# Four PSUM banks in rotation for the scan's stage of a hybrid SSD and attention layer, with eight smaller edits

## The chip, the cores and the metric

The kernel runs on one core of a Trainium2 chip: TensorE (PE) with its weight loads (PEld), VectorE (DVE), ScalarE (ACT), GpSimd (POOL), SyncE (SP, which here only issues DMAs), and 16 DMA engines. PE's sums go to PSUM, eight banks of 128 partitions by 2 KB. The metric is the device time of one execution in microseconds (us); lower is better.

## The reference

One layer of a decoder for 512 tokens of a prompt and 64 of samples (8 sequences of 8 tokens behind 2048 cached positions), 1024 wide, all in float32. Cut to what is computed:

```python
h = x + 0.5 * swiglu(rmsnorm(x, ffn1_norm), ffn1_w_gate, ffn1_w_up, ffn1_w_down)     # D_FF = 2816
xn = rmsnorm(h, mix_norm)
z, xbc, dt_raw, q, k, v, f_raw, g_ssd, g_att = split_combined(xn @ w_in)
y_ssd, h_new, conv_new = ssd_branch(z, xbc, dt_raw, conv_prev, h0, p)
...                      # rms norm of q and k; logf = log_sigmoid(f_raw + b_f)
y_att = fox_attention(q, k_all, v_all, logf_all)      # softmax(q k / 8 + sum of logf), paged past
merged = (sigmoid(g_ssd) * (y_ssd @ w_ssd_proj) + sigmoid(g_att) * (y_att @ w_attn_proj))
h = h + merged @ w_out
h = h + 0.5 * swiglu(rmsnorm(h, ffn2_norm), ffn2_w_gate, ffn2_w_up, ffn2_w_down)
```

`ssd_branch` is a causal convolution over 4 tokens with SiLU, a scan in chunks of 128 tokens (32 heads of 64 in 4 groups, state of 128), a gate SiLU(z), and an rms norm over each group's 512 channels:

```python
y_diag = einsum('bclsgr,bcsgrp->bclgrp', cb[..., None] * decay, xdt)      # cb = C.B within a chunk
states = einsum('bclgn,bclgr,bclgrp->bcgrpn', Bc, exp(acs[:, :, -1:] - acs), xdt)
h_fin, h_prev = lax.scan(step, h_init, (chunk_decay, states))
y_off = einsum('bclgn,bcgrpn,bclgr->bclgrp', Cc, h_prev, exp(acs))
```

The layer also returns keys, values, logf, the scan's final states and the convolution's last inputs.

## The kernel before

Activations lie with channels on the partitions and the 576 tokens (NT; 512 of them NP, the prompt's, and 64 NS, the samples') in the columns, in two halves of 288 (HT). A float32 product is made of three matmuls of a rounded format: weights and activations are split in a high and a low part (`whi`, `wlo`; `xh`, `xl`), and `mm3` issues hi x hi, hi x lo, lo x hi per slice of 128 inputs (L212 to L214). A half tile of a projection from 1024 inputs is 24 such matmuls.

The stages in order of time: the first FFN (from 0 to about 485 us); projections for dt, f, q, k and the rest of the attention's (to 600); attention, with the z gates' projection and others as filling jobs (`beside`, `fill`) between its steps (to 897); the mixing stage (897 to 1376), which is the scan's stage here; then `w_out` and the second FFN.

The mixing stage: `group_in(g)` makes a group's six tiles of B, C and x (`conv_tile`: two half tiles of projection on PE, scaled into `xr` by DVE at L1149 and L1154/L1156, turned at L1162, convolved with `kf` on DVE, L1175). `group_scan(g)` goes over chunk 4 (the samples' tokens) and chunks 0 to 3 with `chunk`, `carry` and `state`. For a chunk, a DMA brings `ab` (cumulated log decays, spread over the partitions, L1314), ACT makes the decay `dk` of it (L1319, L1320), DVE multiplies it by the masked product C.B (`cbm`, L1321), ACT and POOL make the carried part of `ab` (L1323, L1324); PE turns x (L1330) and B (L1337), then multiplies (L1346, L1348); `carry` adds up the state `hst` (L1359 to L1365); `state` multiplies the samples' old states, read back turned from `hTD` (L1373), into `oo`, and `gate` multiplies by z and sums squares on POOL (L1270 to L1274). `oo` is turned at the end into a tile of tag "tr" (L1393), the final state into another (L1404). `halves` splits the result into `ygh` and `ygl`. `group_out(g)` projects it: 16 half tiles of 12 matmuls, each multiplied by the group's norm from `rowscale` (L261 sums squares over partitions on PE) on DVE (`u`, L1425; or L1422) and added to `accs`. Between them stand gate tiles (three behind the first scan, five behind the last) and, first, the attention's projection of `yhl`.

The eight PSUM banks: `accp` has two (tag "acc"); "tr" (turned tiles), "mm" (`sm()`) and "pv" have two each. A tile of a tag takes the slot of the tile two before it, in the order of the program's text. `acc()` gives the accumulator of a projection; while `wide[0]` is true (first FFN, `w_out`, second FFN) every second comes from "pv". In the mixing stage all come from "acc".

The order on each engine is not written out: a scheduler places the instructions by its own times, bound by data, slots and priority (`soon()` raises it); `behind(later, first)` only fixes an order between two instructions and adds no wait. `turns` (L369) turns the samples' old SSM states during the first FFN: a load on SP's queue, four transposes on PE (L385), a copy and a store on ACT's queue. `aside` runs it behind the preparation of the past's log forget values.

Of the kernel before, what the change touches and what calls it, by code (L numbers as in the profile page):

```python
# [23 lines left out]
P = 128  # L24
# [69 lines left out]
def build(ctx, tc, A, O):  # L94
# [113 lines left out]
    def mm3(out, w, xs, half, first=True, last=True):  # L208
        n = len(w)
        for i, ((hi, lo), (xh, xl)) in enumerate(zip(w, xs)):  # L210
            a, b = xh[:, hs(half)], xl[:, hs(half)]
            mm(out, lhsT=hi, rhs=a, start=first and i == 0, stop=False)  # L212
            mm(out, lhsT=hi, rhs=b, start=False, stop=False)  # L213
            mm(out, lhsT=lo, rhs=a, start=False, stop=last and i == n - 1)  # L214

    def hilo(hp, view, tagh, tagl, scale=None, n=NT, bufs=None):

        hi = tl(hp, [P, n], F32R, tag=tagh, bufs=bufs)
        lo = tl(hp, [P, n], F32R, tag=tagl, bufs=bufs)
        if scale is None:  # L220
            act(hi, view, AF.Copy)
            V.tensor_tensor(lo, view, hi.bitcast(F32), ALU.subtract)
        else:
            act(hi, view, AF.Copy, scale=scale)  # L224
            V.scalar_tensor_tensor(lo, view, scale, hi.bitcast(F32), ALU.mult, ALU.subtract)
        return hi, lo
# [45 lines left out]
    class Norm:  # L272


        def __init__(self, wcol, sqp=None, xsp=xp):
            self.wcol, self.xs, self.n, self.sqp, self.xsp = wcol, [], 0, sqp, xsp

        def add(self, h, squares=True):
            k = self.n
            self.xs.append(hilo(self.xsp, h, "xh", "xl", scale=P1[:, self.wcol + k:self.wcol + k + 1]))  # L280
# [88 lines left out]
    def turns(wait):  # L369

        for _ in range(wait):
            yield
        with pool("turn", side="right", reuse_waits="tile") as sp_:
            tiles = []
            for t in range(16):
                for h in range(2):
                    for n in range(len(tiles), min(2 * t + h + 3, 32)):
                        tiles.append(tl(sp_, [P, 4, P], tag="h0", bufs=4))
                        nc.sync.dma_start(out=tiles[n], in_=ap3(A["state_ssm"][0], *place(n % 2, n // 2)))
                    if t + h == 0:  # L380
                        yield
                    h0 = tiles[2 * t + h]
                    ps = tr()
                    for b in range(4):
                        nc.tensor.transpose(ps[:, b * P:(b + 1) * P], h0[:, b, :], ident)  # L385
                    hT = tl(sp_, [P, 512], tag="hT", bufs=3)
                    act(hT, ps, AF.Copy)
                    nc.scalar.dma_start(out=hTD[h, t], in_=hT)
                    yield

# [27 lines left out]
    with pool("h1", reuse_waits="tile") as hp:  # L418
# [41 lines left out]
        with pool("setup2", side="right", reuse_waits="tile") as su:  # L460
# [36 lines left out]
            q.dma_start(out=bb[:32], in_=A["dt_bias"].rearrange("o h -> h o"))  # L497
            q.dma_start(out=bb[32:48], in_=A["b_f"].rearrange("o h -> h o"))
# [3 lines left out]
            q.dma_start(out=al[:32], in_=A["a_log"].rearrange("o h -> h o"))  # L502
# [14 lines left out]
        def aside():  # L517

            with pool("rows", side="right", reuse_waits="tile") as su:

                sc = tl(su, [24, CONV], tag="sc")
                for j in range(3):
                    nc.scalar.dma_start(out=sc[j * B:(j + 1) * B], in_=A["state_conv"][0, :, j, :])
                yield
                yield
                scT = tl(su, [P, 24, 24], tag="scT")
                for j in range(0, 24, 12):
                    t = tr()
                    for i in range(12):
                        nc.tensor.transpose(t[:, i * 24:(i + 1) * 24], sc[:, (j + i) * P:(j + i + 1) * P], ident[:24, :24])  # L530
                    V.tensor_copy(scT[:, j:j + 12, :], t[:, :288].rearrange("p (i c) -> p i c", c=24))
                nc.scalar.dma_start(out=scD, in_=scT)

            with pool("lg", side="right", reuse_waits="tile") as lp:
                pcol = tl(lp, [P, 1], I32, tag="pcol")
                nc.scalar.dma_start(out=pcol, in_=A["page_table"].rearrange("b n -> (b n)").unsqueeze(1))
                lg = tl(lp, [P, P, 16], tag="lg")
                G.indirect_dma_start(out=lg.rearrange("p s h -> p (s h)"), out_offset=None,
                                     in_=A["cache_logf"].rearrange("o n s h -> (o n) (s h)"),
                                     in_offset=bass.IndirectOffsetOnAxis(ap=pcol[:, :1], axis=0))  # L540
                pf = tl(lp, [P, 16, P], tag="pf")
                for h in range(16):
                    V.tensor_tensor_scan(pf[:, h, :], C("one"), lg[:, :, h], 0.0, ALU.mult, ALU.add)
                tot = tl(lp, [P, 16], tag="tot")
                V.tensor_copy(tot, pf[:, :, P - 1])
                page = tl(lp, [P, P], tag="page")
                nc.scalar.dma_start(out=page, in_=A["consts"][:, COFF["page"][0]:COFF["page"][0] + P])
                for _ in range(2):
                    yield
                t = sm()  # L550
                mm(t[:, :16], lhsT=page, rhs=tot, start=True, stop=True)
                st = tl(lp, [P, 16], tag="st")
                V.tensor_copy(st, t[:, :16])

                for h in range(16):
                    G.tensor_tensor(lg.rearrange("p s h -> p (s h)")[:, h * P:(h + 1) * P].rearrange("p (q r u) -> p r q u", q=4, u=4),
                                    pf[:, h, :].rearrange("p (r q u) -> p r q u", q=4, u=4),
                                    st[:, h:h + 1].unsqueeze(2).unsqueeze(3).to_broadcast([P, 8, 4, 4]), ALU.subtract)
                lv = lg.rearrange("p s h -> p (s h)").rearrange("p (h q e) -> p h q e", h=16, q=4)
                for b in range(B):  # L560
                    for q in range(4):
                        nc.scalar.dma_start(out=pastD[b, :, q].rearrange("h g e -> g h e"), in_=lv[b * NPG:(b + 1) * NPG, :, q, :])
            yield from turns(1)
# [12 lines left out]
    wide[0] = False  # L576
# [79 lines left out]
    with pool("att", side="right", reuse_waits="tile") as ap:  # L656
# [147 lines left out]
        G.memset(qz, 0.0)  # L804
        t = sm()
        for j in range(8):
# [3 lines left out]
            mm(t[:, j * NS:(j + 1) * NS], lhsT=sel, rhs=hr[:, NP:], start=True, stop=True)  # L810
# [211 lines left out]
        def beside():  # L1022
            jobs = [(ga, j) for j in range(8)] + [(zc, j) for j in range(16)]
            ahead = ga.get(0)
            for n, (cols, j) in enumerate(jobs):
                w, ahead = ahead, None
                v = tl(mixp, [P, NT], tag="kf", bufs=2)
                for half in range(2):
                    a = acc()
                    for k in range(0, 8, 4):  # L1030
                        mm3(a, w[k:k + 4], xs[k:k + 4], half, first=k == 0, last=k == 4)
# [16 lines left out]
                yield  # L1048

        filler = beside()  # L1050
# [479 lines left out]
```

## Time and profile before

| what | us |
|---|---|
| runs: median of three (lowest, highest) | 1869.34 (1866.79, 1869.46) |
| the profiled execution, its span | 1870.09, 1868.2 |
| PE, its weight loads busy | 1824.8, 1725.6 |
| DVE, ACT, POOL busy | 1064.6, 742.1, 605.7 |
| stage 600 to 897 (attention), PE busy | 297.0, 295.73 |
| stage 1376 to the end, PE busy | 492.2, 486.56 |

The profile lists each engine's instructions with start and length; the groups' names are `out<-in` by the program's tiles, with the line that issued them. The waits view adds up, for one engine, the idle time ahead of a line's instructions and what ended it: us in total, times, longest. The granted clock is 0.995 of full speed in the mean. Matmuls are pipelined and their ends are modelled, so a row can be longer than the distance to the next start.

### The profile page before, as it was taken

The numbers are of one execution on the slowest core, as the hardware profiler recorded it, in microseconds if no ns is written. First come the engines' busy times: TensorE is split into PE (matmuls) and PEld (weight loads), VectorE is DVE, ScalarE is ACT, GpSimd is POOL, SyncE is SP. The second block draws the span as 40 slices with busy tenths as digits, with TensorE's granted clock in tenths as the row PEclk, the third lists the DMA queues.
The fourth block names the chain that finished last, engine by engine and source line by source line (L and its number), as shares of the span: only waits on it lengthen the run. The fifth ranks groups of instructions, "written<-read, shape, count | busy, mean of one in ns | idle before, by whom it ended". The sixth has DMA issues, their size and how long they took to land.

```text
span 1868.2 us, 38772 instructions
## 1 busy us (share of the span) xinstructions
PE 1824.8 (98%) x15335; PEld 1725.6 (92%) x15335; DVE 1064.6 (57%) x2309; ACT 742.1 (40%) x1555; POOL 605.7 (32%) x681
## 2 busy tenths in 40 slices
PE   7999999999999999999999999989999999999998
PEld 7999999999889888888898888878989999999998
DVE  4643334443425677876737969787695454344542
ACT  4333223334323555554426645555433333123322
POOL 0433002312322334442224644746454222002210
PEclk9999999999999999999999999999999999999999
DMA  5354443345525678885356544354472434554342
GB/s 155 121 124 127 130 138 111 119 139 164 141 80 175 190 231 244 237 227 172 91 151 185 155 125 138 103 148 139 135 216 86 124 115 131 145 144 123 109 121 67
DMA packets 297722, 269.71 MB, mean 144 GB/s; under 512 B 55068, under 2 KB 262092, under 8 KB 297388
## 3 DMA queue, kind: packets, MB, share of 16 engines
q1 hardware_dynamic: 229712, 184.16, 35.3%
q10 hardware_dynamic: 57828, 46.10, 8.0%
q0 software_dynamic: 10000, 36.97, 6.4%
q8 instruction: 121, 1.98, 0.5%
q14 instruction: 61, 0.50, 0.1%
HBM read 223.72 MB, written 38.73 MB: 140 GB/s over the span
## 4 chain that ended last, share of the span: by engine, by line
PE 63%; DVE 7%; ACT 1%; DMA 1%; issue 1%; POOL 0%; ACTq 0%; SPq 0%; DVEq 0%; POOLq 0%
PE acc L212 13%; PE acc L214 12%; PE acc L213 12%; PE pv L213 4%; PE pv L214 4%; PE pv L212 4%; PE tr L955 2%; PE tr L942 2%; PE mm L878 1%; DMA ab<-cumD 1%; PE pv L909 1%; PE mm L896 1%; DVE kf L1175 1%; PE tr L982 1%; PE pv L993 1%
## 5 line engine op out<-in xcount | busy, mean ns | idle before, releaser
L177 ACT ACTIVATE whi<-stage 128x512 fp32r<-128x512 f32 (+2 forms) x474 | 294.0, 622 | 714.8 <-PE acc L213 603.7
L212 PE MATMUL acc<-xh,whi 128*128 128x288 f32 x1792 | 541.7, 302 | 7.3 <-DVE xr L1149 4.0
L213 PE MATMUL acc<-xl,whi 128*128 128x288 f32 x1792 | 534.0, 298 | 0.0
L214 PE MATMUL acc<-xh,wlo 128*128 128x288 f32 x1792 | 532.8, 297 | 0.0
L178 DVE TENSOR_TENSOR wlo<-stage,whi 128x512 fp32r<-128x512 f32 (+1 forms) x373 | 263.7, 707 | 269.8 <-ACT whi L177 249.4
L212 PEld LDWEIGHTS acc<-xh,whi 128*128 128x128 f32 x1792 | 339.1, 189 | 14.1 <-DVE xr L1149 5.1
L213 PEld LDWEIGHTS acc<-xl,whi 128*128 128x128 f32 x1792 | 339.2, 189 | 2.9 <-issue 2.7
L214 PEld LDWEIGHTS acc<-xh,wlo 128*128 128x128 f32 x1792 | 338.8, 189 | 1.1 <-issue 0.5
L178 POOL TENSOR_TENSOR wlo<-stage,whi 128x512 fp32r<-128x512 f32 (+1 forms) x101 | 137.9, 1366 | 286.0 <-ACT whi L177 280.1
L345 POOL TENSOR_TENSOR u<-u,s 128x288 f32<-128x288 f32 x88 | 81.5, 926 | 429.0 <-DVE u L344 372.9
L212 PE MATMUL pv<-xh,whi 128*128 128x288 f32 (+1 forms) x720 | 214.1, 298 | 2.3 <-ACT xh L224 2.1
L214 PE MATMUL pv<-xh,wlo 128*128 128x288 f32 (+1 forms) x720 | 213.0, 296 | 0.0
L213 PE MATMUL pv<-xl,whi 128*128 128x288 f32 (+1 forms) x720 | 213.0, 296 | 0.0
L212 PEld LDWEIGHTS pv<-xh,whi 128*128 128x128 f32 (+1 forms) x720 | 135.0, 188 | 3.0 <-ACT xh L224 2.4
L213 PEld LDWEIGHTS pv<-xl,whi 128*128 128x128 f32 (+1 forms) x720 | 134.9, 187 | 1.2
L214 PEld LDWEIGHTS pv<-xh,wlo 128*128 128x128 f32 (+1 forms) x720 | 135.1, 188 | 0.3
L212 PE MATMUL pv<-hh,whi 128*128 128x288 f32 x352 | 106.0, 301 | 0.0
L347 POOL TENSOR_TENSOR hl<-u,hh 128x288 fp32r<-128x288 f32 x88 | 79.3, 903 | 77.5 <-ACT hh L346 77.5
L213 PE MATMUL pv<-hl,whi 128*128 128x288 f32 x352 | 104.3, 296 | 0.0
L212 PE MATMUL acc<-hh,whi 128*128 128x288 f32 x352 | 104.2, 296 | 0.0
L213 PE MATMUL acc<-hl,whi 128*128 128x288 f32 x352 | 104.2, 296 | 0.0
L214 PE MATMUL acc<-hh,wlo 128*128 128x288 f32 x352 | 104.2, 296 | 0.0
(364 smaller groups left out, 3609.8 us busy)
## 6 DMA issues: line engine op xcount, KB each, us to landing
stage<-in_w_in_dram SPq DMA_DIRECT2D x52, 512.0 KB
stage<-in_ffn_w_up_dram SPq DMA_DIRECT2D x44, 512.0 KB
stage<-in_ffn_w_gate_dram SPq DMA_DIRECT2D x43, 512.0 KB
stage<-in_ffn_w_down_dram SPq DMA_DIRECT2D x40, 512.0 KB
h<-in_state_ssm_dram SPq DMA_DIRECT2D x64, 256.0 KB
hTD<-hT ACTq DMA_DIRECT2D x32, 256.0 KB
pb<-pastD SPq DMA_DIRECT2D x32, 256.0 KB
ab<-cumD SPq DMA_DIRECT2D x32, 256.0 KB
```

The costliest lines, as they stand in the source:

```text
L177: act(hi, view, AF.Copy)
L178: e.tensor_tensor(lo, view, hi.bitcast(F32), ALU.subtract)
L212: mm(out, lhsT=hi, rhs=a, start=first and i == 0, stop=False)
L213: mm(out, lhsT=hi, rhs=b, start=False, stop=False)
L214: mm(out, lhsT=lo, rhs=a, start=False, stop=last and i == n - 1)
L345: G.tensor_tensor(u, u, sil[half], ALU.mult)
L347: G.tensor_tensor(hl[:, hs(half)], u, hh[:, hs(half)].bitcast(F32), ALU.subtract)
L878: mm(s[:, :n], lhsT=q, rhs=ks[2 * self.p + e][:, :n], start=hl == 0, stop=hl == 1)
L896: nc.tensor.transpose(t[:, j * P:(j + 1) * P], lt[:, j * P:(j + 1) * P], ident)
L909: mm(self.ob[o:o + 32, i * P:(i + 1) * P], lhsT=vtok[j][:, v0:v0 + 32], rhs=self.pts[e][:, j * P:(j + 1) * P], start=j == 0, stop=j == i)
L942: nc.tensor.transpose(t[:, i * P:(i + 1) * P], kk[:, i, p * P:(p + 1) * P], ident)
L955: mm(s[kv * 32:(kv + 1) * 32, :], lhsT=self.q(kv), rhs=self.kT[kv // 2], start=True, stop=True)
```

## The change

The diff has nine parts. The lines behind it are those of the kernel after.

- `acc()` takes every second accumulator from whatever `wide[0]` names: "pv" in the FFNs and `w_out` as before; "tr" from `group_in(0)` on, for all of the mixing stage. The second half tile of `conv_tile` comes from `acc()` as well.
- The three loads of the biases on ACT's queue go behind the eighth `xh` of the first norm.
- The pool of `turns` is open from the start: its first loads are issued while the past's values are prepared, and the sixteen stores of these values go between the turns, four at a time, each behind the store of a turn.
- In the filling jobs, (tanh + 1) x v, one DVE operation on each of 16 tiles, becomes an addition on ACT and a product on POOL.
- Eight small matmuls for the norm of q go behind given filling matmuls.
- The split of the eight attention outputs goes behind the first, second and third tile that follows, instead of all behind the third's place.
- The transposes of `oo` (first three) go behind the first own product of the chunk two later.
- The last group's result is multiplied by its norm before it is split (`ready`), inside `group_scan(3)`.
- `group_out(3)` then adds its accumulators to `accs` straight from PSUM, without `u`.

```diff
-    wide = [True, 0]
+    wide = [pv, 0]
-    def acc():
+    def acc(full=False):
         wide[1] += 1
-        if wide[0] and wide[1] % 2:
-            return pv()[:, :HT]
-        return tl(accp, [P, 512], tag="acc")[:, :HT]
+        a = wide[0]() if wide[0] and wide[1] % 2 else tl(accp, [P, 512], tag="acc")
+        return a if full else a[:, :HT]
...
-            q.dma_start(out=bb[:32], in_=A["dt_bias"].rearrange("o h -> h o"))
+            behind(q.dma_start(out=bb[:32], in_=A["dt_bias"].rearrange("o h -> h o")), nrm1.insts[7])
...
-    def turns(wait):
-        for _ in range(wait):
-            yield
-        with pool("turn", side="right", reuse_waits="tile") as sp_:
+    def turns(sp_, put):
...
-                    nc.scalar.dma_start(out=hTD[h, t], in_=hT)
+                put.append(nc.scalar.dma_start(out=hTD[h, t], in_=hT))
...
+                    states = turns(tp_, put)
+                    next(states)
...
                     for b in range(B):
+                        yield next(states)
                         for q in range(4):
-                        nc.scalar.dma_start(out=pastD[b, :, q]...
+                            past = nc.scalar.dma_start(out=pastD[b, :, q]...
+                            behind(past, put[-1])
-            yield from turns(1)
+                yield from states
...
-    wide[0] = False
+    wide[0] = None
...
-                    V.scalar_tensor_tensor(v, th, 1.0, v, ALU.add, ALU.mult)
+                    act(th, th, AF.Identity, bias=1.0)
+                    G.tensor_tensor(v, th, v, ALU.mult)
...
+        for j in range(8):
+            behind(qnorms[j], pieces[16 + j // 2])
...
-        full = tl(accp, [P, 512], tag="acc")
-        a = full[:, :HT]
+        a = acc(True)
+        full, a = a, a[:, :HT]
...
+    wide[0] = tr
     nxt = group_in(0)
...
-                for x, first in zip((c, h, V.tensor_tensor(lo, y, hi.bitcast(F32), ALU.subtract)), convs[2]):
+                for x, first in zip((c, h, V.tensor_tensor(lo, y, hi.bitcast(F32), ALU.subtract)), convs[1 + 3 * n // 8]):
                     behind(x, first)
...
-                if c == 2:
+                if c == 2 and g < 3:
                     halves(0)
...
-                nc.tensor.transpose(t[:, i * P:(i + 1) * P], oo[:, i * P:(i + 1) * P], ident)
+                x = nc.tensor.transpose(t[:, i * P:(i + 1) * P], oo[:, i * P:(i + 1) * P], ident)
+                if i < 3:
+                    behind(x, owns[i + 2])
...
+            if g == 3:
+                ready = rowscale(ysq, 1.0 / 512, ysq)
+                for i in range(4):
+                    V.tensor_tensor(xg[:, i, :], xg[:, i, :], ready, ALU.mult)
+                halves(0)
+                halves(1)
...
-                    else:
+                    elif g < 3:
                         u = tl(wo, [P, HT], tag="u", bufs=2)
                         V.tensor_tensor(u, a, rg[:, hs(half)], ALU.mult)
-                        E = V if g == 3 else G
-                        E.tensor_tensor(accs[j][:, hs(half)], accs[j][:, hs(half)], u, ALU.add)
+                        G.tensor_tensor(accs[j][:, hs(half)], accs[j][:, hs(half)], u, ALU.add)
+                    else:
+                        with soon():
+                            V.tensor_tensor(accs[j][:, hs(half)], a, accs[j][:, hs(half)], ALU.add)
...
-        wide[0] = True
+        wide[0] = pv
```

How this moves instructions, at three places. First, PE in the scan of group 0, from the state's product of chunk 2 on. `mm_13004` is that product, `pv_13009` the samples' states, `mm_13039` chunk 3's C.B, and `acc_13511` a half tile of the next group's projection. Before:

```order
L1359 MATMUL mm_13004<-xde_12970,bt_12974 128x512
L1373 MATMUL pv_13009<-hT_13010,cz_12693 32x128 x4
L1373 MATMUL pv_13009<-hT_13016,cz_12693 32x128 x4
L1307 MATMUL mm_13039<-cT_11689,bT_11605 128x128
L213 MATMUL acc_13511<-xl_5169,whi_13504 128x288
L214 MATMUL acc_13511<-xh_5168,wlo_13505 128x288
L212 MATMUL acc_13511<-xh_5266,whi_13504 128x288
```

Now (`mm_13020` the same product, `mm_13055` C.B, `mm_13081` and `mm_13090` the turned x and B, `pv_13094` chunk 3's own products):

```order
L1374 MATMUL mm_13020<-xde_12986,bt_12990 128x512
L1388 MATMUL pv_13025<-hT_13032,cz_12709 32x128
L1320 MATMUL mm_13055<-cT_11705,bT_11621 128x128
L1408 MATMUL tr_13145<-ident_76,oo_12793 128x128
L1343 MATMUL mm_13081<-ident_76,xg_11789 128x128 x4
L1350 MATMUL mm_13090<-ident_76,bT_11621 128x128
L1359 MATMUL pv_13094<-dk_13061,xdt_13086 64x128
L1363 MATMUL pv_13094<-ab_13059,hst_13022 64x128
```

Before, 53 projection matmuls of the next group stand between the two chunks' own products; now none does.

Second, PE at the end of that scan, where `oo` (`tr_13129`, now `tr_13145`) and the final state (`tr_13154`, now `tr_13170`) are turned. Before, the turns stand within the next group's half tiles `acc_13616` and `acc_13671`:

```order
L212 MATMUL acc_13616<-xh_5358,whi_13583 128x288
L1393 MATMUL tr_13129<-ident_76,oo_12777 128x128
L213 MATMUL acc_13616<-xl_5359,whi_13583 128x288
L214 MATMUL acc_13616<-xh_5358,wlo_13584 128x288
L1404 MATMUL tr_13154<-ident_76,hst_13108 128x128 x4
L212 MATMUL acc_13671<-xh_4687,whi_13662 128x288
```

Now `tr_13197`, the first half tile of the next group's first tile, follows them in the same two banks; ahead of the scan's chunk 0 only `acc_13223` and `acc_13307`, 48 matmuls, were computed:

```order
L1374 MATMUL mm_13122<-xde_13088,bt_13092 128x512
L1408 MATMUL tr_13145<-ident_76,oo_12793 128x128
L1422 MATMUL tr_13170<-ident_76,hst_13124 128x128 x4
L212 MATMUL tr_13197<-xh_4717,whi_13186 128x288
L213 MATMUL tr_13197<-xl_4718,whi_13186 128x288
```

The next group's first projection has moved from inside the scan to behind it. The other groups' scans look alike: in the second and third, 48 matmuls stand about chunk 4 and chunk 0, in the last two half tiles of the gates.

Third, ACT near the start, where `xh_138` and `xh_151` are the first two tiles of the FFN's input and `bb`, `al` the biases. Before:

```order
L455 ACTIVATE junk_235,rsx_233<-xin_23_104 128x1024
L497 DMA bb_305<-in_dt_bias_dram 32x1
L224 ACTIVATE xh_138<-h_15_93,P_31_125 128x576
L224 ACTIVATE xh_151<-h_16_94,P_31_125 128x576
L498 DMA bb_305<-in_b_f_dram 16x1
```

Now:

```order
L455 ACTIVATE junk_235,rsx_233<-xin_23_104 128x1024
L225 ACTIVATE xh_138<-h_15_93,P_31_125 128x576
L225 ACTIVATE xh_151<-h_16_94,P_31_125 128x576
L176 ACTIVATE whi_343<-stage_118 128x512
L225 ACTIVATE xh_164<-h_17_95,P_31_125 128x576
```

The three bias loads have gone from there to behind the eighth `xh`.

More of the change, by code (lines that the diff above doesn't have):

```diff
@@ L213, in mm3, with hilo @@
             mm(out, lhsT=hi, rhs=b, start=False, stop=False)
-            mm(out, lhsT=lo, rhs=a, start=False, stop=last and i == n - 1)
-    def hilo(hp, view, tagh, tagl, scale=None, n=NT, bufs=None):
+            end = mm(out, lhsT=lo, rhs=a, start=False, stop=last and i == n - 1)
+        return end
+    def hilo(hp, view, tagh, tagl, scale=None, n=NT, bufs=None, insts=None):
         hi = tl(hp, [P, n], F32R, tag=tagh, bufs=bufs)
@@ L223, in hilo @@
         else:
-            act(hi, view, AF.Copy, scale=scale)
+            h = act(hi, view, AF.Copy, scale=scale)
             V.scalar_tensor_tensor(lo, view, scale, hi.bitcast(F32), ALU.mult, ALU.subtract)
+            if insts is not None:
+                insts.append(h)
         return hi, lo
@@ L517, in aside @@
         def aside():
[L519 to L548, printed above, removed]
-                    yield
[L550 to L562, printed above, removed]
@@ L1345, in chunk @@
                     ov = yb[(r % 2) * 64:(r % 2 + 1) * 64, (r // 2) * n:(r // 2 + 1) * n]
-                    mm(ov, lhsT=xdt[:n, r, :], rhs=dks[r // 4][:n, r % 4, :n], start=True, stop=not 0 < c < 4)
+                    own = mm(ov, lhsT=xdt[:n, r, :], rhs=dks[r // 4][:n, r % 4, :n], start=True, stop=not 0 < c < 4)
+                    if r == 0:
+                        owns.append(own)
                     if 0 < c < 4:
```

91 lines of the change are left out of this document (68 added, 23 removed).

## The prediction

> **What bounds the kernel now.** I read the page's engine rows and its chain first, then busy time by stage.
>
> ```profile
> span 1868.2 us, 38772 instructions
> ...
> PE 1824.8 (98%) x15335; PEld 1725.6 (92%) x15335; DVE 1064.6 (57%) x2309; ACT 742.1 (40%) x1555; POOL 605.7 (32%) x681
> ...
> L212 PE MATMUL acc<-xh,whi 128*128 128x288 f32 x1792 | 541.7, 302 | 7.3 <-DVE xr L1149 4.0
> ```
> ```profile
> 34.00:485.00 451.00, 448.35 (x3399) 446.66 (x3399) 188.53 (x360) 151.72 (x280) 109.81 (x118) 1.00 0.44 127
> ...
> 897.00:990.00 93.00, 88.25 (x643) 86.26 (x643) 51.91 (x87) 31.68 (x53) 25.02 (x39) 0.98 0.45 118
> 990.00:1376.00 386.00, 367.72 (x2999) 331.24 (x2999) 309.85 (x606) 206.71 (x484) 215.42 (x223) 1.00 0.51 144
> ```
>
> TensorE (PE) is busy 1824.8 of 1868.2 us, so no edit to another engine can gain more than it takes out of PE's 43.4 us of idle time. The stage rows give length, then busy time of PE, its weight loads, DVE, ACT and POOL, then the granted clock. From 990 to 1376 us (the four scans with what lies beside them) PE idles 386.00 - 367.72 = 18.3 us; in the first group's input projection, 897 to 990 us, 4.8. Next, what ended PE's waits in the scan stage:
>
> ```profile
> PE acc L212 <- DVE u L1425: 3.8, 4, 1.2
> PE tr L261 <- POOL ssq L1274: 3.2, 1, 3.2
> PE tr L1393 <- ACT oo L1383: 2.1, 1, 2.1
> PE acc L212 <- DVE xr L1149: 1.8, 1, 1.8
> ...
> PE acc L212 <- DVE accs L1422: 0.2, 1, 0.2
> ```
>
> Of the 18.3 us an accumulator's eviction (u, xr) ends a third. None is a wait for a chunk's decay tiles: while they are made, PE computes the next group's projections. The view's 14 rows hold 22 waits. A matmul's row is 302 ns long, though in the dense stretch from 34 to 485 us one starts every 448.35 / 3399 = 0.133 us, so each wait hides another 0.16 us: 18.3 + 22 x 0.16 = **about 22 us** lost in the scan stage before.
>
> **The change: the scan loses its cover.** The order printed above shows it. The scan's own two tiles of turned data (attention of the sample's state, L1393, and the final state, L1404) go through the same two "tr" banks, in program order. In the new order each group's scan ends with them (L1408, L1422), and only then the first half tiles of the next group's projection start. Two half tiles in the "acc" banks, 48 matmuls, run ahead; chunks 0 to 3 stand without filling work. So four banks rotate in the projections, but not across a scan. What PE then waits for is a chunk's own work:
>
> ```profile
> 1310.44 0.45 PE L1346 MATMUL pv<-dk,xdt 128*64 128x128 f32 x4
> ...
> 1314.02 0.49 PE L1307 MATMUL mm<-cT,bT 128*128 128x128 f32 x2
> ```
> ```profile
> L1324 POOL TENSOR_TENSOR ab<-ab,cT 128x512 f32<-128x512 f32 x24 | 33.7, 1406 | 24.2 <-ACT ab L1323 24.2
> ...
> L1270 POOL TENSOR_TENSOR xg<-xg,zt 128x512 f32<-128x512 f32 x16 | 22.8, 1425 | 15.5 <-DVE xg L1350 15.5
> L1364 POOL TENSOR_TENSOR hst<-hst,decb 128x512 f32<-128x512 f32 x12 | 17.1, 1425 | 0.3 <-DVE hst L1365 0.3
> L1273 POOL TENSOR_TENSOR sq<-sq 128x256 f32<-128x256 f32 x16 | 13.5, 844 | 1.5 <-ACT sq L1272 1.5
> L1274 POOL TENSOR_TENSOR ssq<-sq 128x128 f32<-128x128 f32 x16 | 9.5, 595 | 0.7
> ```
> ```profile
> L1321 DVE TENSOR_TENSOR dk<-dk,cbm 128x512 f32<-128x512 f32 x32 | 38.8, 1234 | 4.7 <-ACT dk L1320 4.2
> ...
> L1350 DVE SCALAR_TENSOR_TENSOR xg<-xg,dsk,pv 128x128 f32<-128x128 f32 x64 | 17.9, 341 | 6.8 <-PE pv L1348 6.8
> ...
> L1333 DVE TENSOR_TENSOR xdt<-mm,TT 128x512 f32<-128x512 f32 x16 | 10.9, 680 | 0.0
> ```
>
> PE's own part of a chunk: from its first product to the mask's product, 1314.02 - 1310.44 = 3.6 us, that product itself 0.2, and six turns of a 128x128 tile that I put at 0.1 each (matmuls of twice the columns take 0.133): **4.4 us**. POOL per chunk: 2 x 1.41 + 1.43 + 1.43 + 0.84 + 0.60 = **7.1 us**. DVE: 2 x 1.21 (38.8 / 32) + 4 x 0.28 (17.9 / 64) + 0.68, and two more of 128x512 that I price like this last one (L1335, L1365): **5.6 us**. So a bare chunk is paced by POOL, not by PE. Its preparation can't run far ahead: `ab` and `dk` have three slots, two used per chunk. The slot's way round, as SP's issue and ACT's first use show it:
>
> ```profile
> 1301.06 0.36 SPq L1314 DMA_DIRECT2D ab<-cumD  x1
> ```
> ```profile
> 1305.14 0.99 ACT L1319 ACTIVATE dk<-ab,TT 128x128 f32<-128x128 f32 x3 [1.80 <-DMA ab<-cumD]
> ```
> ```profile
> 989.89 7.18 DMA ab<-cumD
> ```
> ```profile
> 1000.85 0.45 PE L1346 MATMUL pv<-dk,xdt 64*64 64x64 f32 x8 [0.24 <-DVE dk L1321]
> ```
>
> A refill takes 1305.14 - 1301.06 = 4.1 us; behind PE's 4.4 us this makes a loop of 8.5 us if it is fully serial. The bare chunk's period thus lies between 4.4 us (preparation ahead) and 8.5 us; I take **6.8**, nearest POOL's 7.1, since the gate's products may slip behind the next chunk's. The terms:
>
> - Chunks 1 to 3 of four scans: 12 x (6.8 - 4.4) = 28.8. In the last two scans the fill reaches into chunk 1, half of its price each time with the work beside it: 3.5 off (my estimate, 0 to 5). **25.3**; ends 0 (at 4.4) and 49 (at 8.5).
> - Start of scan 0: from the first `ab`'s way (7.18 us from 989.89) to the first own product, which waits for `dk`, are 1000.85 - 989.89 = 11.0 us; the 48 matmuls of cover last 48 x 0.133 = 6.4. 4.6 remain, and chunk 0 is bare too, 2.4: **7**; ends 0 and 11. The other scans' start falls into the filling work.
> - Tails: behind the last chunk the state's output must leave PSUM and be turned and read before a projection may start. The nearest row is the wait of 2.1 us for `oo`; with the DVE reads behind it I take 2.6, four times: **10.4**; ends 4 and 16. Behind the waiting matmul stand both half tiles and the whole next projection on PE's queue, and DVE's xr and the convolution wait for those.
> - Group 3's output weights now carry the norm's scale, so ahead of the gate tiles PE waits (L264) for the sum of squares, as before (the 3.2 us of L261): **3.3**; ends 0 and 5.
> - Other waits inside the projections, an xr or a tt: **2**; ends 0 and 6.
>
> Sum 48 against 22 before: **+26** for the stage. In it group 3's output loses 16 multiplications on DVE (the 3.8 us of waits on `u`), which is part of the 22 that I take as gone.
>
> **The other edits.** The rows:
>
> ```profile
> 13.40 0.33 ACTq L497 DMA_DIRECT2D bb<-in_dt_bias_dram  x1
> 13.78 0.78 ACT L224 ACTIVATE xh<-h,P 128x576 fp32r<-128x576 f32 x1 [1.75 <-DMA stage<-in_ffn_w_gate_dram]
> ```
> ```profile
> PE pv L212 <- ACT xh L224: 2.1, 1, 2.1
> ```
> ```profile
> PE tr L385 <- DMA h<-in_state_ssm_dram: 2.6, 1, 2.6
> ```
> ```profile
> PE acc L212 <- DVE kf L1037: 1.0, 1, 1.0
> ```
> ```profile
> PE acc L212 <- DVE xr L1149: 2.1, 2, 1.7
> ```
>
> - Start: the bias DMA stands ahead of the first `xh` on ACT's queue and holds it to 13.78; put behind the eighth `xh` it frees ACT's 1.75 us of idle time in that row, so 1.7 of PE's 2.1 us should go; the biases are read only behind the first FFN. **-1.7** (0 to -2.1).
> - The state's loads begin earlier, and the past's sixteen stores are spread between the turns: the one wait of 2.6 goes, **-2.8** with the hidden part (0 to -2.8). On SP's queue the loads pass some weight loads, for which no row of this stretch shows a wait; the stores stay on ACT's queue, each behind a turn's store, so nothing newly waits there.
> - The Tanh job: 16 DVE operations become 16 on ACT and 16 on POOL. PE waits 1.0 us there for DVE's kf: **-1.1**. The attention stage beyond it is full on PE, and I count the job and the reordered norms at nothing there (+3 to -3: POOL's product comes later than DVE's did, while PE's next job covers it).
> - 897 to 990 us: four banks, and the splitting of the attention outputs spread over three tiles instead of one. Here there is no scan yet, so the rotation holds: of the 4.8 us idle (5.4 with the hidden part) I take **-5.1** (0 to -5.5).
>
> Sum -10.7. Whole: 26 - 10.7 = **+15.3** on the profiled execution's own time of 1870.1 us (span 1868.2 and 1.9 around it), 1885.4. That execution lies 0.75 us above the median of the runs, so **1885 us**.
>
> **A rule of the Trainium skill.** PE's present waits repeat on accumulators (the rows on u and xr). The Trainium skill, Perfetto Trace Analysis, section Optimization Strategy, says that consistent bubbles on the engine that should be saturated "can mean there isn't enough SBUF/PSUM for the next tile to be allocated"; by it two more banks would take the stage's waits on u and xr, 5.6 us, and with the -10.7 the time would be 1853, which is where rival 1 ends and a part of its chance. That sentence counts banks, not who holds them; here the scan's own tiles hold the added ones.
>
> **The rivals.**
>
> 1. *Preparation runs ahead; faster.* ACT and DVE make a chunk's tiles while PE is still at the last, and a chunk takes 5 us: 12 x 0.6 = 7; tails at 1.2 make 5, the start 3, the rest 2: 17 - 22 - 10.7 = -16, **1854**. For it: the waits view of before has no row on `ab`. Against: three slots, and POOL's 7.1 us. It decides below a period of 5.6 us. 0.16.
> 2. *About the same.* DVE, not POOL, sets the pace (5.6, 5.9 with some weight splitting): 18 - 2, start 5, tails 8, the rest 4: 33 - 22 - 10.7 = 0, **1870**. 0.15.
> 3. *The slots' loop is serial.* Period 8.5: 49 - 3.5 + 11 + 13 + 5 = 75 - 22 - 10.7 = +42, **1912**. For it the 4.1 us of a refill; against, the third slot. 0.14.
> 4. *The clock falls in the bare scans.* Waits of 3 to 4 us would be followed by a few us of slow matmuls. The stage's granted clock is 1.00 although it holds a wait of 3.2 us, so the rows speak against it. If behind the longest wait of each scan the next 3.6 us of matmuls (a chunk's own part, above) ran at half speed, that would add 4 x 3.6 = 14, and 7 if it happened in two of the four: **1892**. 0.05. The Trainium skill, TensorE: Matmul & The Clock Gate, Part 1, has an idle window of about 3.4 us after which the array runs at half rate; the trace's wait of 3.2 us lies just under that, so no run here shows it yet.
>
> That the rotation isn't one of four banks is the forecast itself.
>
> **How the numbers follow.** The forecast, 1877 to 1897 with its terms' smaller ends, has 0.50, the rivals the rest. The range leaves out most of rival 1 and the upper part of rival 3: **1860 to 1910**. Within 0.2% (3.7 us, about what a measurement of this kernel tells from no change): most of rival 2, 0.13. Faster: rival 1 and a little of 2, 0.18. Slower: 0.69.
>
> **What would show it.** In the profile after: the scan's stage longer, with PE idle there near 40 us; waits on `dk`, `ab` or `xdt` at L1359 and L1363, several us per scan; a wait on the turned tiles' readers at the first projection behind each scan; between 897 and 990 nearly no wait; the wait on `xh` near 14 us shorter. Wrong it would be if bare chunks follow each other at 5 us, or if the waits appear on xr rather than on the chunk's tiles.

## The result, and the profile after

The changed kernel takes **1887.33 us** (median of four, 1886.81 to 1888.37) against 1869.4 beside it: ratio 1.0095, interval 1.0082 to 1.0108, so 17.9 us slower. The forecast was 1885 us, 15.3 us slower on its own execution, range 1860 to 1910.

The page of the kernel after: its span, the engines' busy time, and the granted clock in 40 slices of 47 us, in tenths.

```profile
span 1885.9 us, 38848 instructions
...
PE 1827.9 (97%) x15335; PEld 1728.7 (92%) x15335; DVE 1031.0 (55%) x2281; ACT 755.8 (40%) x1571; POOL 623.5 (33%) x697
...
PEclk9999999999999999999997998999999999999999
```

PE's work is the same 15335 matmuls. New is the clock row: it falls to 7 in the slice from 990 us on and to 8 in that from 1131, where the row of before had 9 throughout.

The stages of both kernels, cut at the same places in the program: the end of the first FFN, the first and last product of attention, the last product of the attention's projection, and the last of `w_out`. Columns as in the prediction. Before:

```profile
0.00:461.50 461.50, 449.47 (x3372) 445.89 (x3373) 192.81 (x373) 159.94 (x298) 102.83 (x117) 1.00 0.44 132
461.50:609.80 148.30, 146.87 (x1022) 133.53 (x1020) 61.58 (x138) 47.80 (x89) 40.53 (x41) 0.99 0.49 132
609.80:893.70 283.90, 282.63 (x3635) 241.70 (x3633) 210.76 (x606) 148.31 (x367) 112.65 (x146) 1.00 0.75 217
893.70:989.40 95.70, 90.95 (x680) 88.77 (x670) 52.87 (x89) 31.98 (x53) 25.02 (x39) 0.98 0.48 126
989.40:1429.80 440.40, 421.50 (x3403) 384.71 (x3402) 344.61 (x654) 229.15 (x518) 241.12 (x243) 1.00 0.50 144
```

After:

```profile
0.00:454.90 454.90, 446.60 (x3376) 443.30 (x3377) 192.01 (x373) 160.86 (x299) 103.07 (x118) 1.00 0.46 135
454.90:602.60 147.70, 146.26 (x1017) 132.06 (x1016) 61.52 (x138) 47.02 (x89) 39.60 (x40) 1.00 0.48 130
602.60:889.70 287.10, 284.63 (x3632) 242.28 (x3634) 204.43 (x590) 160.77 (x383) 132.34 (x162) 1.00 0.73 215
889.70:977.20 87.50, 87.50 (x685) 87.06 (x674) 50.44 (x87) 31.45 (x53) 27.36 (x39) 1.00 0.50 126
977.20:1447.90 470.70, 429.47 (x3403) 393.00 (x3403) 320.73 (x643) 230.78 (x518) 237.58 (x243) 0.95 0.47 136
```

By length: -6.6, -0.6, +3.2, -8.2, **+30.3**. In the first group's projection PE is busy 87.50 of 87.50 us: there the four banks do what they can. The whole loss is in the scans' stage, where PE's idle time went from 440.40 - 421.50 = 18.9 to 470.70 - 429.47 = 41.2 us, and its busy time grew by 8.0 us for the same 3403 matmuls. PE's waits there, after:

```profile
PE pv L1359 <- DVE xdt L1346: 19.2, 12, 3.2
PE mm L1320 <- DVE cbm L1308: 4.8, 1, 4.8
PE tr L212 <- ACT x L1424: 4.6, 1, 4.6
PE tr L264 <- POOL ssq L1287: 4.4, 1, 4.4
PE pv L1359 <- DVE dk L1334: 2.1, 1, 2.1
PE tr L1422 <- DVE hst L1380: 1.5, 2, 0.8
```

The waits on u are gone. In their place PE waits 12 times, in nearly every chunk, at the chunk's own product; once 4.8 us for the first scan to begin (behind ACT, which itself waited 3.49 us for the first `ab`), once 4.6 us at a scan's end until the turned state has left its tr bank, once 4.4 us for the sum of squares ahead of the last gates. The prediction named each of these places, though it put 2.6 us behind each of the four scans, and one has 4.6. There ACT, before it read the turned state at 1148.88, had waited for the next `ab` and begun its decay:

```profile
1147.69 1.28 ACT L1332 ACTIVATE dk<-ab,TT 128x128 f32<-128x128 f32 x4 [2.45 <-DMA ab<-cumD]
```

What the prediction had all but ruled out is a fall of the clock. Two microseconds a row, from the wait of 4.8 us at the first scan's start:

```profile
986.00:988.00 2.00, 0.00 (x0) 0.00 (x0) 0.00 (x0) 0.00 (x0) 0.00 (x0) 1.00 0.97 226
988.00:990.00 2.00, 0.03 (x1) 0.04 (x1) 0.57 (x3) 1.75 (x9) 0.00 (x0) 0.54 0.68 254
990.00:992.00 2.00, 1.28 (x3) 0.69 (x3) 1.30 (x5) 2.00 (x10) 0.00 (x0) 0.50 0.54 115
992.00:994.00 2.00, 1.94 (x20) 1.64 (x20) 1.40 (x5) 1.72 (x5) 0.00 (x0) 0.50 0.95 279
```

About 3 us into the wait the clock goes to 0.50. The state's product (two 128x512 matmuls) shows what that does: in the first scan's chunks 0 and 2, by the timeline,

```profile
998.75 2.07 PE L1374 MATMUL mm<-xde,bt 128*128 128x512 f32 x2
...
1019.85 1.13 PE L1374 MATMUL mm<-xde,bt 128*128 128x512 f32 x2
```

2.07 against 1.13 us. By this line's rows the first scan's chunks follow at 11.0, 10.2 and 9.8 us; those of the other three scans at 6.0 to 8.2, 7.0 in the mean of nine.

### The profile page after: what moved, and what is told of

It reads as the page before. It is cut to its first block, busy times and chain, and to the rows that moved or that the text cites. A ratio compares the mean times of both kernels' runs of the same rounds, so it can differ in the third digit from the quotient of the medians.

```text
span 1885.9 us, 38848 instructions
## 1 busy us (share of the span) xinstructions
PE 1827.9 (97%) x15335; PEld 1728.7 (92%) x15335; DVE 1031.0 (55%) x2281; ACT 755.8 (40%) x1571; POOL 623.5 (33%) x697
## 5 line engine op out<-in xcount | busy, mean ns | idle before, releaser
L212 PE MATMUL acc<-xh,whi 128*128 128x288 f32 x1536 | 461.0, 300 | 0.2 <-DVE qy L669 0.2
L214 PE MATMUL acc<-xh,wlo 128*128 128x288 f32 x1536 | 454.2, 296 | 0.0
L213 PE MATMUL acc<-xl,whi 128*128 128x288 f32 x1536 | 453.8, 295 | 0.0
L212 PEld LDWEIGHTS acc<-xh,whi 128*128 128x128 f32 x1536 | 288.3, 188 | 2.2 <-issue 0.8
L213 PEld LDWEIGHTS acc<-xl,whi 128*128 128x128 f32 x1536 | 288.4, 188 | 1.2 <-issue 0.8
L214 PEld LDWEIGHTS acc<-xh,wlo 128*128 128x128 f32 x1536 | 288.0, 188 | 1.3 <-issue 0.8
L214 PE MATMUL pv<-hh,wlo 128*128 128x288 f32 x352 | 103.7, 295 | 0.0
```

Source lines behind the costliest of these rows:

```text
L214: end = mm(out, lhsT=lo, rhs=a, start=False, stop=last and i == n - 1)
```

## The experiments

Theory A: the scan's turned tiles hold the tr banks, so the scan loses its cover (the forecast). Rivals: another edit does it (B), or accumulators in tr cost by themselves (C). Ratios are to the kernel before on the same chip, which took between 1868.5 and 1872.3 us in the median; 0.001 is 1.9 us.

**Acc banks alone in the mixing stage, all other edits kept.**

```diff
-    wide[0] = tr
     nxt = group_in(0)
```

> The changed kernel with every accumulator of the mixing stage from the two acc banks, as before the change; all eight other edits stay. Theory A (the scan's two turned tiles hold the tr banks, so the accumulators cannot run ahead and the scan loses its cover): the scans are covered again, the 30 us that the stage from the end of the attention's projection to the end of w_out gained in length go, and the time is 1869.4 - 12 + 0 to 4 (part of the 8.3 us won in the first group's projection came from the four banks) = 1857 to 1862 us. Rival B (one of the other edits, such as group 3's norm inside the scan or the turns of oo set behind later chunks, lengthened the stage): 1875 us or more.

1864.78 us, ratio 0.9983 (0.9970 to 0.9996); just above theory A's range, since the first projection took 93.5 us against 87.5 in the changed kernel: 6 of the 8.2 us won there need the four banks. The stage is 436.0 us long, 34.7 less than with the rotation:

```profile
984.50:1420.50 436.00, 419.82 (x3403) 382.78 (x3402) 335.04 (x642) 229.15 (x518) 243.65 (x243) 1.00 0.50 145
```

B falls: with every other edit in place the stage is shorter than the 440.4 us before the change.

**The rotation alone, put into the kernel before.**

```diff
-    wide = [True, 0]
+    wide = [pv, 0]
...
+    wide[0] = tr
     nxt = group_in(0)
```

> The kernel before with the rotation alone: every second accumulator of the mixing stage from tr, nothing else changed. Theory A: the loss of the stage comes with it, so 1869.4 + 22 to 30 = 1891 to 1900 us. Rival B (the loss is that of another edit): 1860 to 1870 us.

1886.01 us, ratio 1.0100 (1.0074 to 1.0127), +17.5 on 1868.5. Theory A's range began at 1891, as it had left out what the rotation wins ahead of the scans:

```profile
893.10:980.60 87.50, 87.50 (x682) 87.07 (x671) 49.54 (x87) 31.18 (x53) 29.93 (x39) 1.00 0.50 128
980.60:1447.00 466.40, 426.81 (x3403) 391.02 (x3402) 330.62 (x655) 230.10 (x518) 236.74 (x243) 0.96 0.48 138
```

Against the kernel before, -8.2 there and +26.0 in the stage make +17.8. The rotation by itself makes the loss.

**The scan's two turned tiles in the mm banks, rotation kept.**

```diff
-            t = tr()
+            t = sm()
             for i in range(4):
                 x = nc.tensor.transpose(t[:, i * P:(i + 1) * P], oo[...], ident)
...
-            t = tr()
+            t = sm()
             for i in range(4):
                 nc.tensor.transpose(t[:, i * P:(i + 1) * P], hst[...], ident)
```

> The changed kernel, rotation kept, but the scan's two turned tiles (oo and the final state) in the mm banks instead of tr. Theory A: nothing of the scan stands between the accumulators in tr, the next group's projection runs inside the scan again, and the time is 1850 to 1860 us, with few waits on xdt at the chunk's own product (under 5 us in the stage against 19.2). Rival C (taking accumulators from tr is what costs, whoever else uses these banks, since the norm's tile of group_out stands there too): 1878 us or more. Theory A is also hurt if the time comes out above 1870.

1873.12 us, ratio 1.0030 (1.0016 to 1.0045): between acc banks alone and the full rotation, and above the 1870 us from which theory A was to be hurt. The order on PE has the projections inside the first three scans again, and the chunks of the first follow at 13 to 16 us, near the 12 to 16 of the covered scan of before. So these two tiles are what had uncovered them. But the stage is still 17.6 us longer than with acc banks alone, and more waits on xdt remain than the 5 us expected:

```profile
979.30:1432.90 453.60, 424.70 (x3404) 389.01 (x3404) 335.12 (x643) 228.00 (x518) 246.81 (x243) 0.97 0.49 141
```
```profile
PE pv L1359 <- DVE xdt L1346: 10.7, 6, 3.1
```

Of the 10.7 us, 8.2 are the last scan's. There a third tile stands in tr ahead of the gates: the norm's, which this change had moved into `group_scan(3)`.

**The norm's tile in mm as well, so that tr holds accumulators only.**

```diff
         with soon():
-            t = tr()
+            t = sm() if wide[0] is tr else tr()
```

> As the run with the turned tiles in the mm banks, and the norm's tile (the sum over partitions) in mm as well, so that in the mixing stage tr holds accumulators and nothing else. In that run the last scan was still bare, since the norm's tile stood in tr ahead of the gate tiles, and the clock was at half speed for 24 us. Theory A: the last scan is covered by the gates, its 3 waits of 2.6 to 3.3 us and the low clock there go, 1860 to 1866 us. Rival C (accumulators in tr cost for another reason): 1871 to 1875 us as before.

1872.51 us, ratio 1.0000 (0.9985 to 1.0015): inside rival C's range, not theory A's, and still no better than the acc banks alone.

```profile
983.30:1433.60 450.30, 423.97 (x3405) 389.10 (x3404) 341.05 (x643) 227.41 (x518) 245.53 (x243) 0.97 0.50 142
```
```profile
PE tr L212 <- ACT ygh L1296: 6.3, 1, 6.3
PE mm L1343 <- DVE xg L1191: 4.5, 2, 3.8
PE pv L1359 <- DVE xdt L1346: 4.2, 5, 1.9
```

The last scan is covered (xdt 4.2 us in all), and the gates are now used up when the norm's chain (sum, root, product, split into `ygh`) runs: PE waits 6.3 us for it. Likewise PE is through a group's projection sooner and then waits 3.8 us for the convolved x (L1191) that the scan turns first. The waits now end on DVE's and ACT's chains. The stage took 470.7 us with the rotation, 453.6 and 450.3 with the scan's tiles out of tr, and 436.0 with acc banks alone. So A is shown for some 20 of the 34.7 us between the first and the last. The other 14 stay while accumulators are taken from tr, as C says; what makes them (those longer chains, the clock at 0.97 with them, or the turned tiles now in mm) was not tried apart. Even unblocked, four banks won nothing in this stage.

**Does the low clock cost anything?** The two half tiles that run ahead of the first scan are computed twice:

```diff
-        mm3(a, w, xs, 1)
+        for _ in range(2 if ct in (17, 21) else 1):
+            mm3(a, w, xs, 1)
```

> The changed kernel, with the two half tiles that run ahead of the first group's scan computed twice over (48 more matmuls, 6.4 us of PE work; the second pass starts the sum anew). In the profile of the change PE waits 4.8 us at the start of that scan, the granted clock is 0.61 to 0.73 from 985 to 1020 us, and the scan's chunks follow at 10 us against 6 to 8 in the other scans. Theory D (the wait lowered the clock, and the low clock stretches the scan): the wait is filled, the clock stays near 1.00 through the scan, chunks follow at 7 us, and the time is 1878 to 1884 us although there is more work. Rival E (the scan is paced by the other engines alone and the low clock costs nothing): 6.4 us more work less 4.8 us of filled wait, 1887 to 1891 us.

1878.77 us, ratio 1.0063 (1.0040 to 1.0086), under the changed kernel's by 6.0 us by the ratios and 8.6 by the medians. The first scan with its start, in the changed kernel and then in this one:

```profile
977.20:1032.00 54.80, 38.18 (x290) 27.42 (x290) 29.52 (x75) 31.85 (x98) 21.98 (x21) 0.75 0.60 170
```
```profile
979.60:1026.00 46.40, 35.26 (x338) 28.50 (x337) 26.78 (x68) 29.94 (x93) 21.34 (x20) 0.96 0.70 187
```

48 more matmuls, and 8.4 us less time: the clock is 0.96 instead of 0.75, and the state's products, from the first to the last of the scan, follow at 6.6, 7.1 and 7.2 us:

```profile
1000.51 1.13 PE L1375 MATMUL mm<-xde,bt 128*128 128x512 f32 x2
...
1021.35 1.12 PE L1375 MATMUL mm<-xde,bt 128*128 128x512 f32 x2 [0.65 <-ACT bt L1354]
```

Behind the first scan the two kernels' stages differ by 0.9 us. Theory D holds: useless work in a wait paid for itself.

**What paces a bare chunk?** First, POOL's two sums of squares taken out. This kernel leaves out three quarters of the squares that the group's norm needs, and ACT squares a quarter of what it did:

```diff
-                act(q, yv, AF.Square)
-                G.tensor_tensor(q[:, :2, :], q[:, :2, :], q[:, 2:, :], ALU.add)
-                G.tensor_tensor(ysq[:, o0:o0 + n], q[:, 0, :], q[:, 1, :], ALU.add)
+                act(ysq[:, o0:o0 + n], yv[:, 0, :], AF.Square)
```

> The changed kernel without POOL's two sums of squares per chunk: it leaves out three quarters of the sum that the group's norm divides by (ACT writes the squares of the first 128 channels straight to ssq). POOL's work of a chunk falls from 7.1 to 5.7 us. Theory H (POOL paces the bare chunk): the period of chunks 1 to 3 falls by 1 us or more, the wait for the sum of squares ahead of the last gates (4.4 us) by half, and the time is 1865 to 1877 us. Theory G or any pace set by DMA and DVE's order: the period stays within 0.4 us, only the wait ahead of the last gates shortens by 1.4 us, 1882 to 1887 us.

1883.12 us, ratio 1.0064 (1.0046 to 1.0081). The mean period of the last three scans is 6.6 us against 7.0, while POOL lost 1.4; it is 6.8 in the runs with the rotation alone and with the half tiles twice, where POOL's work is the same, so half of the 0.4 may be spread. The wait ahead of the gates fell from 4.4 to 2.0, by more than the 1.4 that POOL lost. H, POOL as the pace, falls in the size it was given.

Then four slots for `ab`, with one fewer for `hT` to make room:

```diff
-                    ab = tl(wk, [P, 4, P], tag="ab", bufs=3)
+                    ab = tl(wk, [P, 4, P], tag="ab", bufs=4)
...
-                hT = tl(wk, [P, 512], tag="hT", bufs=4)
+                hT = tl(wk, [P, 512], tag="hT", bufs=3)
```

> The changed kernel with four slots for ab instead of three, and three for the read-back states (hT) instead of four, which makes the room. Theory G (the way of an ab slot, from PE's last use over a DMA of 4 to 5 us to ACT, sets the pace of a bare chunk): the mean period of chunks 1 to 3 in the last three scans falls from 7.0 us to 6.2 or less, in the first from 10 to 8, and the time to 1868 to 1880 us. Theory H of the prediction (POOL's 7.1 us per chunk set the pace): the period stays within 0.3 us of 7.0, and the time is 1884 to 1889 us.

1893.88 us, ratio 1.0118 (1.0101 to 1.0136): the period rose to 8.8 us, against both theories. POOL's work is unchanged, so H is not what moved it. G's loop did get shorter: in the bare chunks of the last three scans ACT waited 2.7 us for `ab` in all, where it had waited 14.4 in the changed kernel. So in this run the slot's way does not set the pace. What changed is DVE's order, where both of a chunk's masked products `dk` now stand ahead of xdt (in the third scan, at a mean clock of 0.89 there):

```profile
1228.81 2.93 DVE L1334 TENSOR_TENSOR dk<-dk,cbm 128x512 f32<-128x512 f32 x2
```

The fewer slots for `hT` were not tried apart. In the changed kernel one `dk` stands there, between two chunks' products in the second scan:

```profile
1127.53 0.69 DVE L1380 TENSOR_TENSOR hst<-hst,mm 128x512 f32<-128x512 f32 x1 [1.70 <-PE mm L1374]
1128.13 0.28 DVE L1322 TENSOR_TENSOR cbm<-mm,cst 128x128 f32<-128x128 f32 x1
1128.52 0.92 DVE L1334 TENSOR_TENSOR dk<-dk,cbm 128x512 f32<-128x512 f32 x1
1129.36 1.11 DVE L1365 SCALAR_TENSOR_TENSOR xg<-xg,dsk,pv 128x128 f32<-128x128 f32 x4
1130.39 0.68 DVE L1346 TENSOR_TENSOR xdt<-mm,TT 128x512 f32<-128x512 f32 x1
```

Behind PE's state product come five steps in order on DVE, 3.5 us from 1127.53 to 1131.07, and only the last one, xdt, releases PE's next products (at 1131.22). With PE's own 3 to 4 us this ring makes some 7 us. That it sets the pace is argued from these rows and from the run with four slots, where DVE's part from hst to xdt took 4.8 us (1227.50 to 1232.34); no run made the ring shorter.

**The rotation for the first group alone**, acc banks from the first scan on:

```diff
         late = iter(range(8))
+        wide[0] = None
         for g in range(4):
```

> The changed kernel with the rotation through tr for the first group's projection and the attention's projection alone, and the two acc banks from the first scan on. Theory A (the four banks help where no scan holds tr, and cost only across scans): the run with acc banks alone gave 1864.8 and took 93.5 us from the end of attention to the end of the attention's projection, against 87.4 with four banks; 6 us less, 1857 to 1861 us, the fastest so far. Rival F (the 6 us won there are lost again in the first scan, which then starts earlier than its decay tiles arrive): 1863 to 1867 us.

1863.23 us, ratio 0.9952 (0.9938 to 0.9965). On that chip the kernel before took 1872.31, so it and the acc banks alone were run again side by side:

> The run with the acc banks alone once more, beside the next three on one chip, since the chips so far differ by 4 us in the kernel before. As measured there: 0.998 of before, 1865 us where before takes 1868.5.

> The run with the rotation for the first group alone, on the same chip as the run with acc banks alone. Theory A: 5 to 6 us below that run, as the shorter first projection (87.4 against 93.5 us) says. Rival F (the first scan gives it back): within 2 us of it; the profiles so far showed the stage behind it 6.5 us longer than with acc banks alone, with 10 us of half clock.

1864.43 us (0.9962, 0.9950 to 0.9974) and 1863.36 us (0.9948, 0.9932 to 0.9963): 1.1 us apart, which the intervals don't separate. Acc banks alone, then the rotation for the first group:

```profile
893.50:986.70 93.20, 89.80 (x683) 87.32 (x671) 51.04 (x89) 31.89 (x53) 24.58 (x39) 1.00 0.47 127
986.70:1424.10 437.40, 420.63 (x3402) 383.83 (x3401) 335.31 (x642) 229.27 (x518) 242.14 (x243) 1.00 0.50 145
```
```profile
895.20:982.60 87.40, 87.40 (x680) 86.96 (x669) 49.45 (x87) 31.43 (x53) 27.77 (x39) 1.00 0.51 131
982.60:1424.60 442.00, 421.64 (x3404) 385.26 (x3403) 336.13 (x643) 230.00 (x518) 244.45 (x243) 0.99 0.50 144
```

5.8 us won in the projection, 4.6 lost behind it: rival F. Of these, 3.4 lie ahead of the first scan's first state product, which comes 1004.71 - 982.6 = 22.1 us into the stage against 1005.39 - 986.7 = 18.7. PE arrives there sooner, but then waits 2.5 us for the scan to begin, behind ACT, which itself waits 3.0 us for the first `ab`.

**The Tanh job back on DVE**, with the rotation for the first group and with acc banks alone:

```diff
-                    act(th, th, AF.Identity, bias=1.0)
-                    G.tensor_tensor(v, th, v, ALU.mult)
+                    V.scalar_tensor_tensor(v, th, 1.0, v, ALU.add, ALU.mult)
```

> The rotation for the first group alone, and the filling job's (tanh + 1) x v back on DVE as one operation. The attention stage took 283.9 us before and 282.7 with the rotation alone, but 285.6 to 290.8 in all runs that had the job on ACT and POOL. Theory K (that job's place costs the attention 3 to 5 us): attention at 283 to 285 us, time 2 to 5 us below the run with the rotation for the first group alone. Rival L (the length of attention varies for another reason, such as the placing of q's norm): within 1.5 us of it.

> The same with the acc banks alone: the job back on DVE, no rotation in the mixing stage. Theory K: 2 to 5 us below the run with the acc banks alone; rival L: within 1.5 us of it.

1861.93 us (0.9946, 0.9930 to 0.9963) and 1868.07 us (0.9978, 0.9967 to 0.9989): 1.4 below and 3.6 above their partners. K falls: the attention stage took 288 and 290 us in their traces, where K asked for 283 to 285. (The 3.6 lie outside rival L's 1.5 as well.) The attention stage took 285.6 us and 290.5 us in two executions of one and the same kernel (acc banks alone), so its +3.2 in the changed kernel can't be put down to an edit.

The rotation for the first group alone, with or without the Tanh job on DVE, is the fastest version here by its median, 0.5% under the kernel before and, by the ratios, 1.5% under the changed one; acc banks alone, side by side with it, are not told apart from it.

## Why the prediction was right, step by step

- **The scans lose their cover; +26 forecast, +30.3 measured.** Right: the rotation alone gives +26.0 in the stage, and without it the loss is gone. That the scan's own tiles in tr do it is shown for some 20 us, by the runs with these tiles elsewhere; for the rest of the loss the forecast had no step. PE's idle time, forecast near 40 us, is 41.2.
- **The terms.** Chunks 25.3: the waits on xdt and dk are 21.3. Start 7: 4.8. Tails 10.4: 4.6 + 1.5 and some 1 us more. Last gates 3.3: 4.4. Other waits 2: 3.4. So chunks, start and tails were each 2 to 4 us too dear, the other two about 1 us too cheap. The period of 6.8 us: 7.0 in three scans, while the first scan's, 10.3, was far above. With the forecast's 0.16 us hidden in each of the 27 waits, 41.2 + 4.3 = 45.5 us stand against its 48, which is 23.5 above its 22 for before. The other 6.8 of the 30.3 us had no term; the slow matmuls below are what the runs show for them.
- **A reading of before.** The forecast found no wait for a chunk's decay tiles there. Its view holds two on dk and two on xdt at L1346, 0.6 and 1.2 us in all; beside 21.3 after, they change nothing.
- **What was wrong in it: the clock.** Rival 4 got 0.05 because "the stage's granted clock is 1.00 although it holds a wait of 3.2 us". That row was a mean over 386 us. Cut finer, the trace of before shows the same fall behind that very wait:

```profile
1240.00:1242.00 2.00, 2.00 (x10) 1.75 (x9) 2.00 (x4) 0.00 (x0) 1.25 (x2) 0.57 1.15 343
1242.00:1244.00 2.00, 2.00 (x11) 2.00 (x11) 1.58 (x4) 0.74 (x2) 0.00 (x0) 0.58 0.43 146
```

  (2 x 0.43 + 2 x 0.42) / 0.5 = 3.4 us at half speed, 0.4% of the stage, which a mean of two digits can't show. So the forecast was also wrong that no run showed such a fall yet. In the changed kernel's stage the mean is 0.95: 0.05 x 470.7 / 0.5, about 47 us at half speed. The busy time grew by 8.0 us net; with the first scan's wait filled, that scan was 8.4 us shorter. So rival 4's slow matmuls came beside the forecast's waits, not in their place: they belonged in the sum, which put them at nothing. That the total came as near as 15.3 to 17.9 is partly luck: the waits in the stage were put 2.5 us too dear and the other edits' gain 1.5 too small. The Trainium skill, TensorE: Matmul & The Clock Gate, Part 1, which has half rate after an idle window of about 3.4 us, was the right warning: the trace agrees roughly, with 0.50 granted about 3 us into the wait of 4.8 us. In the trace of before a wait of 3.2 us was enough, and there the fall came about 0.9 us behind its end at 1239.34, if the half speed of the two rows lies in one piece.
- **POOL as the pace.** Wrong as a cause: the waits are on DVE's xdt, and 1.4 us less on POOL took 0.4 off the period. The number came out by luck: DVE's ring with PE, which by the argument above sets the pace, takes about as long.
- **The other edits, -10.7 forecast, -12.2 measured** (-6.6 - 0.6 + 3.2 - 8.2). Start and state loads -4.5 forecast, -6.6 measured; the first projection -5.1 against -8.2, of which the rotation alone gives all, though 2.2 come without it; the Tanh job nothing that can be told from the spread of attention.
- **The rule on bubbles.** The Trainium skill, Perfetto Trace Analysis, section Optimization Strategy, says that consistent bubbles can mean too little PSUM for the next tile. The traces agree where nothing else used the banks: in the first projection 3.4 us of idle time remained with acc banks alone (93.20 - 89.80), and none with four. Across the scans they do not, as the forecast argued.

## What to carry to other kernels

Banks that rotate in program order are shared with every tile in that order: before accumulators borrow a pool, look which long-lived tile stands between two of them, for all that follows waits for it, and the engine loses the work that covered another stage's latency. Here, with PE nearly full, unblocked banks only moved the waits to the next chain, so ask what that chain can deliver. And price a new wait of several microseconds on TensorE with the slow matmuls behind it; read the clock in windows as short as the wait.

## What the runs showed of the hardware

Shorter waits than the one of 4.8 us were followed by a low clock too. In the first scan of the changed kernel, around a wait of 1.9 us for xdt that ends at 1015.5:

```profile
1012.00:1014.00 2.00, 1.61 (x24) 1.15 (x16) 1.52 (x3) 1.97 (x6) 1.32 (x2) 0.99 0.46 82
1014.00:1016.00 2.00, 0.51 (x6) 0.51 (x8) 2.00 (x4) 2.00 (x7) 1.57 (x1) 0.87 0.88 310
1016.00:1018.00 2.00, 2.00 (x20) 1.67 (x21) 0.04 (x1) 1.37 (x4) 1.28 (x2) 0.50 0.14 40
```

The clock was back at 0.99 before it and is 0.50 again behind it. Another wait of 1.9 us, which ends at 1139.5, was not followed by a fall (1.00 from 1138 to 1142); what parts the two is not shown. A second thing that few would expect: 48 matmuls that compute nothing new made the kernel 6 to 9 us faster, by keeping PE at work through one wait.
